# A four-layer trunk on one core: the delta-rule layer's matmuls put in one fixed order

## The chip, the core and the metric

The kernel runs on one core of a Trainium2 chip. The metric is the device time of one execution in microseconds (us), from launch to the last output. The profile is of one execution; its span runs from the first to the last instruction.

Engines: PE is TensorE (matmuls; PEld its weight loads), DVE is VectorE, ACT is ScalarE, POOL is GpSimd, SP is SyncE, which here only issues DMAs. Each engine takes its own instructions in order and waits on semaphores for what other engines make.

## The reference

Four residual layers on x (256 tokens by 1024, float32): pooling mixer, gated delta rule, latent attention, pooling mixer again; a final RMS norm. What matters here is layer 1, the delta-rule layer (8 heads, keys of 128, values of 256):

```
proj = h @ w_in                       # 1024 -> q 1024, k 1024, v 2048, gate 2048, b 8, a 8
qkv = silu(causal_depthwise_conv(qkv, conv_w))      # 4 taps
q, k = l2norm(q) * dk**-0.5, l2norm(k)
beta = sigmoid(b); g = cumsum(-exp(a_log) * softplus(a + dt_bias))   # within a chunk
L = strict_lower((k*beta) @ k.T * decay)
sol = triangular_solve(I + L, [v*beta, k*beta*exp(g)])
# per chunk, with a state per head:
v_new = u - w @ state
o = (q*exp(g)) @ state + (q @ k.T * decay) @ v_new
state = state * exp(g_last) + k_dec.T @ v_new
y = (rmsnorm(o, norm_g) * silu(gate)) @ w_out
```

The reference uses chunks of 64; the kernel uses two chunks of 128 tokens (t = 0 and 1) and so one state per head.

## The kernel before

**Strips.** A projection is done in strips of 512 output columns (`project`, L131). Weights come through SP in pieces of 512 KB (two 128-row slices of a strip, one "unit", so four units to a strip of w_in; three buffers `raw`). `weights` (L97) splits each slice into a rounded high part on ACT (`whi`, L117) and the rest on DVE or POOL (`wlo`, L119; the argument `pool` says which slices go to POOL); nine of each are kept. Each product is then three matmuls: high by high, high by low, low by high (`mm3`, L126 to L129, for strips whose output has channels on the partitions, 96 matmuls of 256 columns; L167 for strips with tokens on the partitions, 48 matmuls of 512 columns). I call the first kind C strips (q, k, v) and the second R strips (the gates).

**The delta-rule layer** (`gdn_layer`, L535). There are twelve strips: gates g0 to g3 (R), keys k0 and k1, queries q0 and q1, values v0 to v3 (C). A C strip's result lies in two PSUM banks. `conv` (L628) applies the taps: one scaled copy on ACT and three multiply-adds on DVE for each of four channel groups, then a SiLU on ACT. For keys and queries `channels` (L659) then transposes on PE (L675), squares on ACT (L678) and sums on DVE (L679, `ssq`); POOL makes the norms (`power`, L657). `against` (L683) multiplies keys by keys (to LT) or keys by queries (to attnT) for four heads and both chunks (16 matmul records, L688), and DVE scales them into SBUF (L692) by the decay DT, which DVE and ACT make (L618, L626) from a broadcast by DMA.

**The inverse.** `substitution` (L712) inverts the 32 by 32 diagonal blocks of all heads: eight DMAs gather them out of LT (`d_l`, L718), one brings them back with a block to a partition (`Lb`, L721), POOL does 31 steps of a product and a subtraction (L726, L730), one DMA writes the result (`d_t`, L732) and eight put it in T (L736). All these DMAs are on SP's queue, between the weights. `inverses` (L787) then joins the blocks: `pairs` (L806, L812) and `whole` (L820, L824, L830) for each chunk, PE and DVE in turns.

**The heads.** `news` (L839) makes the first chunk's values; then eight heads go through five stages (L870 to L926): `state`, `unseen`, `second`, `outputs`, `finished`. `outputs` is followed by a norm on ACT (L209) and POOL (L900 to L903) and a product with the gate on DVE (L906); `finished` transposes on PE (L915) for the output projection (`layer_out`, L348).

**The order.** The program text sets the order by the list

```
order = "g0 k0 d a0 g1 k1 a1 s q0 v0 i v1 v2 q1 g2 u0 v3 u1 g3".split()
```

(d the decays, a `lower`, s `substitution`, i `inverses`, u `news`), followed by the heads' steps and the output projection. But a planner that simulates the engines decides each engine's order: it may take any instruction whose inputs it believes to be ready, and so it mixes strips, inverses and heads. Where it believes a result to be earlier than the chip has it, the instruction that needs it stands at the head of its engine's queue and all behind it wait. `later` adds an order on one engine by hand. Buffer counts of most pools are also the planner's.

Of the kernel before, what the change touches and what calls it, by code (L numbers as in the profile page):

```python
# [42 lines left out]
def trunk(ctx: ExitStack, tc: tile.TileContext, x, positions, norm_g, pool_w_in, pool_w_grp,  # L43
# [48 lines left out]

    mark = {}
# [32 lines left out]
    def mm3(o, lhs, rhs, start, stop):  # L126
        nc.tensor.matmul(o, lhsT=lhs[0], rhs=rhs[0], start=start, stop=False)  # L127
        nc.tensor.matmul(o, lhsT=lhs[0], rhs=rhs[1], start=False, stop=False)  # L128
        nc.tensor.matmul(o, lhsT=lhs[1], rhs=rhs[0], start=False, stop=stop)  # L129

    def project(src, ks, act, cols=CW, chan=False, tail=0, done=None, cuts=1,  # L131
                where="acc", pool=()):
# [13 lines left out]
        if chan:  # L146
            banks = [bank(acc if where == "acc" else aux, where) for _ in range(2)]
            for k0, n in ks:
                parts = unit(k0, n)
                for j in range(n):  # L150
                    k = k0 + j
                    for c in range(cols // P):
# [3 lines left out]
                            k == last and c % 2 == 1)  # L156
            return banks
# [3 lines left out]
        def rows(t, c, k0, n, parts):  # L161
            o, sl = banks[t][c][:, :width], slice(c * width, (c + 1) * width)
            for x, y in ((0, 0), (0, 1), (1, 0)) if n == 1 else ((0, None), (1, 0)):
                for j in range(n):
                    k = k0 + j
                    for z in (0, 1) if y is None else (y,):
                        nc.tensor.matmul(o, lhsT=act(k, t * P, P)[x], rhs=parts[j][z][:, sl],  # L167
# [4 lines left out]
        for u, (k0, n) in enumerate(ks):  # L172
# [7 lines left out]
            for t in range(NT):  # L180
                for c in range(cuts):
                    for one in now:
                        rows(t, c, *one)
                    if done and u == len(ks) - 1:
                        done(t, c, banks[t][c][:, :width])
        return [b[0] for b in banks]
# [82 lines left out]
    for _ in range(WARM):  # L269
        nc.tensor.transpose(ps[:, :P], ident, ident)  # L270
# [41 lines left out]
    class LayerIn(Normed):  # L312
# [6 lines left out]
        def feed(self, t):  # L319
            for c, h in enumerate(self.rest(t)):  # L320
                ps = bank(tps, "tp")
                for b in range(4):
                    nc.tensor.transpose(ps[:, b * P:(b + 1) * P], h[:, b * P:(b + 1) * P], ident)
# [24 lines left out]
    def layer_out(w, yT, ks, i):  # L348
# [7 lines left out]
        project(cols_of(w, 0), ks, yT, done=lambda t, c, ps: done(t, 0, ps))  # L356
# [19 lines left out]
    def turn_params():  # L376
# [13 lines left out]
        nc.tensor.transpose(ps[:, :P], rows, ident)  # L390
# [20 lines left out]
    def pool_layer(i, j, hT):  # L411
# [37 lines left out]
        def mixed(g, pT, gs):  # L449
# [15 lines left out]
            for a in range(2):  # L465
                ps = bank(tps, "tp")
                for b in range(2):
                    for t in range(NT):
                        c = 2 * a + b
                        nc.tensor.transpose(ps[:, b * S + t * P:b * S + (t + 1) * P],  # L470
# [25 lines left out]
    def gdn_setup():  # L496
# [21 lines left out]
        nc.tensor.transpose(ps[:, :P], crow, ident)  # L518
# [16 lines left out]
    def gdn_layer(i, j, hT):  # L535
# [15 lines left out]
        def gate(vi):  # L551
            banks = project(cols_of(w_in, 2 * GDN_QK + GDN_V + vi * CW), units(KD), hT,
                            pool=((0, 4), (7,), (3, 7), (7,))[vi])
# [5 lines left out]
        order = "g0 k0 d a0 g1 k1 a1 s q0 v0 i v1 v2 q1 g2 u0 v3 u1 g3".split()  # L559
        while order[0][0] == "g":  # L560
            gate(int(order.pop(0)[1]))
# [3 lines left out]
        for k in range(KD):  # L565
            for x, part in enumerate(hT(k, 0, S)):
                nc.tensor.matmul(ps[:32, :S], lhsT=bws[:, k].rearrange("p a c -> p (a c)"),
# [4 lines left out]
        for t in range(NT):  # L572
            nc.tensor.transpose(ps[:, t * 32:(t + 1) * 32], ba[:, t * P:(t + 1) * P],
# [23 lines left out]
        nc.tensor.matmul(ps[:, :M], lhsT=utri, rhs=flat(lga), start=True, stop=True)  # L597
# [655 lines left out]
```

## Time and profile before

| what | before |
|---|---|
| median of 3 runs | 859.88 us (859.83 to 860.01) |
| the profiled execution's own time | 859.14 us |
| its span | 857.4 us |
| mean granted TensorE clock | 0.990 |

The delta-rule layer's matmuls lie from about 178 to 403 us of the span. In the lists of the profile a row is: line, engine, operation, output<-inputs, shape, count, then times. In timelines the first two numbers are start and length in us; of merged rows the length is the time covered. In brackets stands how long the engine had been idle and what released it. "PEclk" is the TensorE clock that was granted, 1.00 being full speed.

### The profile page before, as it was taken

Reading aid. Unit: us, or ns where it says so; the run is one execution under the profiler, and the core shown is the slowest. Engines: PE = TensorE matmul, PEld = TensorE weight load, DVE = VectorE, ACT = ScalarE, POOL = GpSimd, SP = SyncE. Lnnn points to the kernel's source line nnn. Section 1 sums busy time; section 2 is a strip of 40 time slices with the busy share of each in tenths; the row PEclk is TensorE's granted clock in tenths of the full one; section 3 lists DMA queues with packets and bytes.
Section 4 is the critical chain, followed back from the end, with each engine's and each line's share of the span. In section 5 each row is a group of like instructions: output and inputs, shape, how many; then the busy total and the mean of one; then the engine's idle time right before and its main releaser. Section 6 shows DMA issues by size and latency. Waiting matters only on the chain.

```text
span 857.4 us, 16137 instructions
## 1 busy us (share of the span) xinstructions
PE 835.0 (97%) x5967; PEld 778.7 (91%) x5967; DVE 591.2 (69%) x1138; ACT 488.2 (57%) x1007; POOL 155.7 (18%) x292
## 2 busy tenths in 40 slices
PE   7999999999999969999999999999999999999996
PEld 6999998988999959888979998999989989999986
DVE  4589776456989665656577659778767668866852
ACT  5565555467857435555565654566555476555542
POOL 4000000233248941022212002000000210000012
PEclk9999999999999989999999999999999999999999
DMA  6765556546555462222547676743652547565551
GB/s 199 249 188 188 178 189 213 180 148 206 188 160 176 134 168 102 75 74 99 173 147 215 201 165 172 196 132 95 171 167 79 173 149 218 175 192 183 187 200 50
DMA packets 111288, 140.43 MB, mean 164 GB/s; under 512 B 23340, under 2 KB 53224, under 8 KB 111208
## 3 DMA queue, kind: packets, MB, share of 16 engines
q1 hardware_dynamic: 109056, 138.17, 53.1%
q8 instruction: 47, 0.77, 0.4%
q0 software_dynamic: 320, 1.06, 0.3%
q10 hardware_dynamic: 1832, 0.16, 0.2%
q14 instruction: 33, 0.27, 0.1%
HBM read 137.79 MB, written 1.58 MB: 163 GB/s over the span
## 4 chain that ended last, share of the span: by engine, by line
PE 85%; POOL 7%; DVE 2%; DMA 2%; issue 2%; ACT 1%; SPq 1%; POOLq 0%; ACTq 0%; DVEq 0%
PE acc L167 34%; PE acc L127 12%; PE acc L128 12%; PE acc L129 12%; POOL Tb L730 2%; POOL pr L726 2%; PE aux L127 2%; PE aux L128 2%; PE aux L129 2%; DVE h L303 1%; DMA gain<-in_norm_g_dram 1%; PE aux L688 1%; ACT junk L209 1%; PE aux L806 1%; PE tp L1165 1%
## 5 line engine op out<-in xcount | busy, mean ns | idle before, releaser
L119 DVE TENSOR_TENSOR wlo<-raw,whi 128x512 fp32r<-128x512 f32 (+1 forms) x491 | 338.6, 712 | 163.2 <-ACT whi L117 160.9
L117 ACT CAST whi<-raw 128x512 fp32r<-128x512 f32 (+1 forms) x508 | 301.4, 617 | 261.8 <-PE acc L167 89.8
L127 PE MATMUL acc<-hTh,whi 128*128 128x256 f32 x832 | 235.3, 283 | 1.0 <-DVE cv L636 1.0
L128 PE MATMUL acc<-hTl,whi 128*128 128x256 f32 x832 | 235.8, 283 | 0.0
L129 PE MATMUL acc<-hTh,wlo 128*128 128x256 f32 x832 | 234.7, 282 | 0.0
L127 PEld LDWEIGHTS acc<-hTh,whi 128*128 128x128 f32 x832 | 157.7, 190 | 1.8 <-issue 1.4
L128 PEld LDWEIGHTS acc<-hTl,whi 128*128 128x128 f32 x832 | 157.6, 189 | 0.4
L129 PEld LDWEIGHTS acc<-hTh,wlo 128*128 128x128 f32 x832 | 157.5, 189 | 0.2
L167 PE MATMUL acc<-wlo,yTh 128*128 128x256 f32 (+1 forms) x384 | 116.2, 319 | 0.0
L167 PE MATMUL acc<-whi,yTh 128*128 128x256 f32 (+1 forms) x384 | 116.2, 323 | 0.0
L167 PE MATMUL acc<-whi,yTl 128*128 128x256 f32 (+1 forms) x384 | 92.4, 321 | 0.0
L167 PEld LDWEIGHTS acc<-wlo,yTh 128*128 128x128 f32 x384 | 72.0, 188 | 5.0
L167 PEld LDWEIGHTS acc<-whi,yTh 128*128 128x128 f32 x384 | 71.9, 188 | 5.2
L167 PEld LDWEIGHTS acc<-whi,yTl 128*128 128x128 f32 x384 | 63.1, 188 | 5.6
L291 POOL TENSOR_TENSOR hg<-x,gain 128x256 f32<-128x256 f32 x18 | 14.8, 832 | 259.1 <-DVE x L353 257.4
L167 PE MATMUL acc<-wlo,hTh 128*128 128x512 f32 (+1 forms) x144 | 55.9, 394 | 0.4 <-DVE wlo L119 0.2
L167 PE MATMUL acc<-whi,hTh 128*128 128x512 f32 (+1 forms) x144 | 55.5, 393 | 0.7 <-ACT hTh L195 0.7
L167 PE MATMUL acc<-whi,hTl 128*128 128x512 f32 (+1 forms) x144 | 45.4, 388 | 0.0
L119 POOL TENSOR_TENSOR wlo<-raw,whi 128x512 fp32r<-128x512 f32 x17 | 23.1, 1360 | 70.2 <-ACT whi L117 70.2
L434 POOL COPY win<-u 128x4 f32<-128x4 f32 x8 | 2.8, 354 | 177.0 <-ACT u L428 177.0
L167 PEld LDWEIGHTS acc<-wlo,hTh 128*128 128x128 f32 x144 | 27.3, 190 | 6.8 <-DVE wlo L119 1.7
L167 PEld LDWEIGHTS acc<-whi,hTh 128*128 128x128 f32 x144 | 27.3, 190 | 6.8 <-ACT hTh L195 1.7
(337 smaller groups left out, 1443.3 us busy)
## 6 DMA issues: line engine op xcount, KB each, us to landing
raw<-in_pool_w_in_dram SPq DMA_DIRECT2D x60, 512.0 KB, 4.4
raw<-in_gdn_w_in_dram SPq DMA_DIRECT2D x48, 512.0 KB, 3.9
raw<-in_pool_w_out_dram SPq DMA_DIRECT2D x32, 512.0 KB, 3.7
raw<-in_mla_w_in_dram SPq DMA_DIRECT2D x24, 512.0 KB, 4.4
raw<-in_mla_w_uq_dram SPq DMA_DIRECT2D x36, 256.0 KB, 3.8
raw<-in_pool_w_grp_dram SPq DMA_DIRECT2D x16, 512.0 KB, 4.2
raw<-in_gdn_w_out_dram SPq DMA_DIRECT2D x16, 512.0 KB, 3.5
raw<-in_mla_w_ukv_dram SPq DMA_DIRECT2D x32, 256.0 KB, 3.4
```

Of the source, the lines that this page charges most:

```text
L117: a = nc.scalar.copy(hi, v)
L119: b = e.tensor_tensor(out=lo, in0=v, in1=hi.bitcast(F32), op=ALU.subtract)
L127: nc.tensor.matmul(o, lhsT=lhs[0], rhs=rhs[0], start=start, stop=False)
L128: nc.tensor.matmul(o, lhsT=lhs[0], rhs=rhs[1], start=False, stop=False)
L129: nc.tensor.matmul(o, lhsT=lhs[1], rhs=rhs[0], start=False, stop=stop)
L167: nc.tensor.matmul(o, lhsT=act(k, t * P, P)[x], rhs=parts[j][z][:, sl], start=k == first and x == z == 0, stop=k == last and x == 1)
L209: nc.scalar.activation(junk[:, :n], src, AF.Square, scale=scale, accum_out=o)
L291: nc.gpsimd.tensor_tensor(out=self.early[t, a], in0=xs[t][:, sl], in1=self.g[:, sl], op=ALU.mult)
L303: nc.vector.scalar_tensor_tensor(out=h[:, cut:], in0=xs[t][:, sl], scalar=r[:, 0:1], in1=self.g[:, sl], op0=ALU.mult, op1=ALU.mult)
L688: nc.tensor.matmul(ps[:, b], lhsT=kT[hf][:, b, tt], rhs=rhs[hf][:, b, tt], start=True, stop=True)
L726: nc.gpsimd.tensor_tensor(out=pv, op=ALU.mult, in0=Lb[:, r, r + 1:, None].to_broadcast([M * Q, n, c]), in1=Tb[:, r:r + 1, :c].to_broadcast ...
L730: nc.gpsimd.tensor_tensor(out=tv, in0=tv, in1=pv, op=ALU.subtract)
```

## The change

From the second key strip on, every PE instruction of the layer, up to the first half of its output projection, is kept in the order of the program text (`pinned`, `keep_in_program_order`: each is placed behind the one traced before it on PE). The text's order is new and written out by unit: `project` is now a generator, and after each unit of a strip it runs the steps given for that place. The other engines' orders are still the planner's, and so is PE's outside the layer.

```diff
+    def matmul(*args, **opts):
+        ins = nc.tensor.matmul(*args, **opts)
+        return tc.keep_in_program_order(ins) if pinned["on"] else ins
...
+    def project(*args, between=(), **opts):
+
+        steps = strip(*args, **opts)
+        between = list(between)
+        while True:
+            try:
+                next(steps)
+            except StopIteration as end:
+                return end.value
+            side = between.pop(0) if between else None
+            for one in side or ():
+                one()
...
-        order = "g0 k0 d a0 g1 k1 a1 s q0 v0 i v1 v2 q1 g2 u0 v3 u1 g3".split()
...
+        keys(0)
+        decays()
+        pinned["on"] = True
+        keys(1, (), (), [do(key_norms, 0)])
+        queries(0, [do(lower, 0)], [do(key_norms, 1)], [do(lower, 1), substitution])
+        gate(1, (), [do(query_norms, 0)], [do(scored, 0)])
+        values(0)
+        queries(1, (), (), [do(values_turned, 0)])
+        gate(2, (), [do(query_norms, 1)], [do(scored, 1)])
+        values(1)
+        values(2, (), [do(values_turned, 1), inverses], [inv("pairs", 0)], [inv("pairs", 1)])
+        values(3, [inv("joined", 0)], [inv("joined", 1), inv("turned", 0)],
+               [do(values_turned, 2), inv("whole", 0), inv("turned", 1)],
+               [inv("last", 0), inv("whole", 1)])
+        gate(3, [inv("last", 1), do(news, 0)], [do(step, 0), do(values_turned, 3)],
+             [do(news, 1), do(step, 1)], [do(step, 2)])
+        for n in range(3, 6):
+            step(n)
+        return layer_out(gdn_w_out[j], yT, units(POOL_W // P), i,
+                         [[do(step, n)] for n in range(6, H + len(stages) - 1)])
```

`values(2, (), [x], [y], [z])` reads: strip v2, nothing after its first unit, x after the second, y after the third, z after the fourth. The old steps are cut into pieces that can be placed: `channels` into `channels` (strip, taps, SiLU) and `squares` (transposes, squares, sums; called by `key_norms` and `query_norms`, which also do POOL's norms); `queries` further into `scored` (the products with the keys); `values` into `values` and `values_turned`; `pairs` into `pairs` and `joined`; `whole` into `turned`, `whole`, `last`. `step(n)` does the five stages for heads n to n-4. `layer_out` puts steps 6 to 11 behind the first six units of its first half and then sets `pinned` off. `g0` and `k0` come before, in the planner's order.

The slices whose low part POOL makes also change:

```diff
-                            pool=((0, 4), (7,), (3, 7), (7,))[vi])
+                            pool=() if vi else (0, 4), between=between)
...
-                            pool=() if which else (0, 4))
+                            pool=() if which else (0, 2, 4, 6), between=between)
...
-                            pool=((1, 3, 5, 7), (3, 7), (), ())[vi])
+                            between=between)
```

The first is the gates, the second the keys (`which` is 0 for them), the third the values. Of the 96 slices of w_in POOL had sixteen and has ten; after k1 it has none. No arithmetic changes.

More of the change, by code (lines that the diff above doesn't have):

```diff
@@ L354, in done @@
             part_done(t, a, n)
-        project(cols_of(w, 0), ks, yT, done=lambda t, c, ps: done(t, 0, ps))
+        project(cols_of(w, 0), ks, yT, done=lambda t, c, ps: done(t, 0, ps), between=between)
+        pinned["on"] = False
         with later(mark["sp"]):
@@ L389, in turn_params @@
         ps = bank(tps, "tp")
-        nc.tensor.transpose(ps[:, :P], rows, ident)
+        transpose(ps[:, :P], rows, ident)
         nc.vector.tensor_copy(colsT, ps[:, :P])
@@ L853, in news @@
                                          scale=s1[:, 0, h:h + 1])
-        steps = {"g": gate, "k": keys, "a": lower, "q": queries, "v": values, "u": news}
-        once = {"s": substitution, "d": decays, "i": inverses}
-        for name in order:
-            if name in once:
-                once[name]()
-            else:
-                steps[name[0]](int(name[1]))
         yT = Split("yT", POOL_W // P)
```

160 lines of the change are left out of this document (90 added, 70 removed).

## The prediction

> **What bounds the kernel now.** I read the page first, then who waited for whom on PE inside the layer, then the windows around the longest wait, and last the timelines of PE, SP, POOL and DVE there.
>
> ```profile
> span 857.4 us, 16137 instructions
> PE 835.0 (97%) x5967; PEld 778.7 (91%) x5967; DVE 591.2 (69%) x1138; ACT 488.2 (57%) x1007; POOL 155.7 (18%) x292
> ```
>
> PE is busy for 97% of the span, so a new order can only win what PE loses by waiting or by a slower clock. In the layer's stretch, 180 to 403 us, the list of PE's waits has two rows:
>
> ```profile
> PE aux L806 <- DMA T<-d_t: 7.4, 1, 7.4
> PE acc L127 <- DVE cv L636: 1.0, 1, 1.0
> ```
>
> PE's timeline has both places, and the windows show the clock after the long one (their columns: PE, PEld, DVE, ACT, POOL, then PEclk):
>
> ```profile
> 303.87 0.36 PE L127 MATMUL acc<-hTh,whi 128*128 128x256 f32 x1 [0.97 <-DVE cv L636]
> 316.09 3.65 PE L806 MATMUL aux<-T,LT 128*128 128x64 f32 x16 [7.36 <-DMA T<-d_t]
> 326.57 1.89 PE L806 MATMUL aux<-T,LT 128*128 128x64 f32 x16
> ...
> 315.00:320.00 5.00, 3.91 (x18) 3.94 (x19) 3.38 (x4) 2.60 (x6) 0.00 (x0) 0.50 0.59 117
> 320.00:325.00 5.00, 5.00 (x29) 5.00 (x28) 1.50 (x3) 1.89 (x5) 0.00 (x0) 0.58 0.64 241
> 325.00:330.00 5.00, 5.00 (x50) 5.00 (x50) 2.67 (x5) 3.71 (x9) 0.00 (x0) 1.00 0.00 0
> ```
>
> `pairs` of the first chunk stood at the head of PE's queue for 7.36 us until T had landed. A good part of v3, the whole of g3 and the heads stood behind it, though they need no T or not yet. After the wait the clock was half: the sixteen matmuls of `pairs` took 3.65 us, and 1.89 us the second time. Half speed from 316.09 to 320 and a mean of 0.58 to 325 lose 0.5 x 3.91 + 0.42 x 5 = 4.05 us. So what can be won is 7.36 + 4.05 + 0.97 = 12.4 us. The profiled execution took 859.14 us, 1.74 more than its span and 0.74 (0.09%) less than the median, 859.88; I sum against 859.14. The floor is 859.1 - 12.4 = 846.7. About 0.2% (1.7 us) is what a measurement of this kernel can tell from no change.
>
> **The chain that T comes from,** on PE (its last product of keys by keys), SP and POOL:
>
> ```profile
> 238.10 0.61 PE L688 MATMUL aux<-kqT 128*128 128x128 f32 x4
> ...
> 256.10 0.53 SPq L721 DMA_DIRECT2D Lb<-d_l  x1
> 310.12 0.47 SPq L732 DMA_DIRECT2D d_t<-Tb  x1
> ...
> 259.78 0.23 POOL L726 TENSOR_TENSOR pr<-Lb,Tb 64x31 f32<-64x31 f32 x1 [1.25 <-DMA Lb<-d_l]
> 265.04 2.08 POOL L657 TENSOR_TENSOR rq<-rq,halves 128x8 f32<-128x8 f32 x1
> 293.13 1.28 POOL L119 TENSOR_TENSOR wlo<-raw,whi 128x512 fp32r<-128x512 f32 x1
> 298.81 1.29 POOL L119 TENSOR_TENSOR wlo<-raw,whi 128x512 fp32r<-128x512 f32 x1
> 309.85 0.24 POOL L730 TENSOR_TENSOR Tb<-Tb,pr 64x31 f32<-64x31 f32 x1
> 334.58 1.29 POOL L754 TENSOR_TENSOR Gb<-Gb,kqT 128x512 f32<-128x512 f32 x1 [1.02 <-ACT kqT L669]
> ```
>
> From the end of lower(1)'s matmuls (238.71) to T (316.09) are 77.4 us; 50.3 of them are POOL's (259.78 to 310.09), with foreign work between: one set of query norms (the `rq` row stands for it) and two weight slices. The change takes the slices out of the chain (-1.28 - 1.29). In the new order the second set of query norms falls into it in place of the first (no difference), with the 1.29 us product L754, which here came after. So the chain is 77.4 - 2.6 + 1.3 = 76.1 us.
>
> **What covers it after the change.** Rates of PE: a C strip, an R strip, sixteen matmuls of `against` (to the next row's start), eight transposes (the same):
>
> ```profile
> 270.00:280.00 10.00, 10.00 (x87) 10.00 (x86) 10.00 (x20) 6.39 (x13) 9.14 (x12) 1.00 0.61 179
> ...
> 204.60:213.00 8.40, 8.40 (x37) 6.75 (x36) 1.00 0.59 205
> ...
> 354.64 2.05 PE L688 MATMUL aux<-kqT 128*128 128x128 f32 x16
> 356.53 0.81 PE L847 MATMUL aux<-vR,U 128*128 128x256 f32 x3
> ...
> 352.55 1.09 PE L778 MATMUL tp<-ident,vc 128*128 128x128 f32 x8
> 353.57 0.62 PE L830 MATMUL aux<-U,X 64*64 64x64 f32 x7
> ```
>
> A C strip is 96 x 10/87 = 11.0 us, an R strip 48 x 8.4/37 = 10.9, `against` for four heads 1.89, eight transposes 1.02. Between lower(1) and pairs(0) the fixed order has: a quarter of q0, v0, q1, v1 and three quarters of v2, which is four C strips (44.0); g1 and g2 (21.8); `scored` twice (3.8); `query_norms` twice and `values_turned` twice (4.1). That is 73.7 us. T then comes 76.1 - 73.7 = 2.4 us late. PE waits 2.4 us there, with v2's last unit, v3 and the inverse queued behind. A gap of 0.97 us (above) left the clock at full rate, one of 7.36 did not; I take 2.4 with the short one and charge nothing for the clock.
>
> [...]
>
> Bounds of the wait: 0 (T early wins nothing, since PE is then busy), and about 7 where DVE scales LT later than now.
>
> **Keys back to back.** Both key strips and q0 now follow each other, with no R strip between, and PE must find each SiLU done at a fixed place. DVE's rows (twelve taps at the first row's rate, weight slices, half the decays, sum and copy for two heads, LT for four heads):
>
> ```profile
> 230.75 2.42 DVE L636 SCALAR_TENSOR_TENSOR cv<-acc,tap,cv 128x254 f32<-128x254 f32 x6
> 218.95 1.90 DVE L119 TENSOR_TENSOR wlo<-raw,whi 128x512 fp32r<-128x512 f32 x3
> 214.14 2.19 DVE L618 SCALAR_TENSOR_TENSOR DT<-Gb,G,maskT 128x128 f32<-128x128 f32 x8 [2.33 <-DMA Gb<-d_g]
> 220.75 0.68 DVE L679 TENSOR_REDUCE ssq<-sq 128x4 f32<-128x512 f32 x1
> 221.35 0.42 DVE L681 COPY ktok<-tp 128x256 f32<-128x256 f32 x1
> 225.88 2.16 DVE L692 SCALAR_TENSOR_TENSOR LT<-aux,s,DT 128x128 f32<-128x128 f32 x8
> ```
>
> A strip's taps are 4.8 us, a slice 0.63, the decays 4.4, a half's sums and copies 2.2, LT for four heads 2.2. While k1 runs (11.0 + 1.0 us) DVE has k0's taps, four slices of k1 and, early, four of q0: 4.8 + 8 x 0.63 = 9.8, which fits. After k1's end PE has two units and lower(0), 2 x 2.75 + 1.9 = 7.4 us, before it needs k1's SiLU for key_norms(1). If DVE takes k1's taps first, 4.8 fits; if the decays and the first sums go ahead, 4.4 + 2.2 + 4.8 = 11.4, and PE waits 4.0. I take 1.5, nearer to the first, since the decays can wait for LT. This wait delays chain and cover alike, so it adds. query_norms(0) comes two R units (5.4 us) after q0, with 4.8 of taps and up to 2.2 + 2.2 of sums and LT ahead of them on DVE: a wait of 0 to 4. It lies under the chain and comes off the 2.4 us at T; I add nothing.
>
> POOL now takes eight slices of the keys instead of four; the trace has one beside a slice of DVE:
>
> ```profile
> 242.31 1.30 POOL L119 TENSOR_TENSOR wlo<-raw,whi 128x512 fp32r<-128x512 f32 x1
> 242.39 1.76 DVE L119 TENSOR_TENSOR wlo<-raw,whi 128x512 fp32r<-128x512 f32 x1
> ```
>
> DVE's slice took 1.76 us instead of 0.63. For k1 that is at worst 4 x 1.1 = 4.5 us more on DVE, against 2 x 0.63 = 1.3 saved by the two more slices that POOL takes there; DVE's slack of 2.2 us and the early slices of q0 take most of it, so it stays within the 0 to 4 above.
>
> [...]
>
> **The heads.** Steps 3 to 5 have no unit between. `outputs` of a head must pass ACT, POOL and DVE before `finished`:
>
> ```profile
> 364.73 0.59 PE L895 MATMUL aux<-v,attnT 128*128 128x256 f32 x2
> 367.75 0.60 PE L869 MATMUL aux<-u,ktok 128*128 128x256 f32 x2
> ...
> 368.06 0.88 DVE L906 SCALAR_TENSOR_TENSOR yg<-aux,or,gsg 128x256 f32<-128x256 f32 x2 [1.35 <-POOL or L903]
> ```
>
> From 365.32 to 368.94 are 3.6 us. PE's work between, the next step's first four stages, is 2.6 (365.17 to 367.75 holds the same six products). One wait of 1.0 us in step 4; step 5 then has 0.4 more work between and that wait, and waits no more. The other steps have units of 2.75 us between. The inverse's pieces each have one or two units for their trip over DVE or ACT, so they add none. PE's instructions are the same in number, and the 0.97 us wait goes with the two POOL slices that held weights back.
>
> **Sum.** 859.1 - 12.4 + 1.5 (keys) + 2.4 (T) + 1.0 (heads) = 851.6 us.
>
> **The rivals.**
> - *The T wait stays.* The planner has no cause to hurry LT if it thinks POOL's chain shorter than it is, as it did before (it placed `pairs` 7.4 us early). If q0's taps (4.8 us) go ahead of LT(1), T is 2.4 + 4.8 = 7.2 us late and the clock's 4.05 is lost again: 851.6 + 4.8 + 4.05 = 860.4, no change. For it: two thirds of the chain is POOL's, and the planner took T for earlier than it was. Against: LT(1) needs only 2.2 us of DVE, and q0's taps become ready a unit (2.75 us) after lower(1). If half of that delay comes, 4.8 us late with half the clock's loss, it is 851.6 + 2.4 + 2.0 = 856.0.
> - *Slower: q0's taps as late as now.* Before, q0's taps and SiLU ran so:
>
> ```profile
> 241.88 0.48 DVE L636 SCALAR_TENSOR_TENSOR cv<-acc,tap,cv 128x255 f32<-128x255 f32 x1 [1.32 <-ACT cv L633]
> 254.85 0.47 DVE L636 SCALAR_TENSOR_TENSOR cv<-acc,tap,cv 128x253 f32<-128x253 f32 x1
> 255.86 1.33 ACT L669 ACTIVATE kqT<-cv 128x256 f32<-128x256 f32 x4
> ```
>
> From the first tap to the last SiLU are 15.3 us. Nothing waited then, as PE had other strips; in the fixed order query_norms(0) waits at 5.4 us, so 9.9 us with g1's second half behind it, and the clock halves (4.05). That hides the T wait: 859.1 - 12.4 + 1.5 + 9.9 + 4.05 + 1.0 = 863.2. It decides where the waits pass 12.4 us in all. Against it: those 15.3 us held twelve taps, LT and slices that nobody hurried; DVE's own sum is under 10.
> - *POOL's slices of the keys hold DVE up in full:* 3.2 us more at key_norms, 851.6 + 3.2 = 854.8. The pair of rows speaks for it, DVE's slack in k1 against; 0.12 of the forecast's 0.60, in whose own range it lies.
> - *The order binds nothing*, the planner having had nearly this one: 859. Unlikely, as the strips change places.
>
> **How the numbers follow.** The forecast has 0.60, with a range of its own from 847 to 855.5 (keys 0 to 4, T 0 to 3, heads 0 to 1.5). The T wait by half (856.0) 0.13; in full, with the order that binds nothing, 0.10, within 0.2%; slower 0.14; better than 847 0.03. Faster 0.76, same 0.10, slower 0.14. Left out above 860 are most of the slower cases and some of the full T wait; the range is 846.7 to 860.
>
> **What would show it.** [...] Wrong if a wait on kqT or on T is over 5 us and PEclk falls to 0.5 behind it. POOL's chain from the first `pr` to the last `Tb` should be about 49 us with no weight slice in it, and d_t should leave some 11 us sooner than now, since g1's strip (10.9 us) no longer lies ahead of lower(1).

## The result, and the profile after

| what | before | after |
|---|---|---|
| median | 859.86 us (859.09 to 860.01, 4 runs) | 885.7 us (884.45 to 886.94, 4 runs) |
| ratio to before, 95% interval | | 1.0308 (1.0293 to 1.0322) |
| span of the profiled execution | 857.4 us | 885.2 us |
| its mean granted TensorE clock | 0.990 | 0.975 |

The change makes the kernel 25.8 us slower. (One execution each of two kernels of the experiments, e6_late2 with 1656.44 us and e18_fit with 4475.5 us, stood far outside all others; the ratios leave it out, and the medians would move by under 0.2 us without it.) The page's head has nearly as many instructions as before, and PE busy for 9.9 us more (half clock counts as busy) in a span that is 27.8 us longer:

```profile
span 885.2 us, 16118 instructions
PE 844.9 (95%) x5967; PEld 784.7 (89%) x5967; DVE 594.7 (67%) x1144; ACT 494.6 (56%) x1009; POOL 144.1 (16%) x286
```

PE's waits between 180 and 410 us (total, times, longest):

```profile
PE tp L100 <- ACT kqT L694: 19.7, 9, 6.2
PE tp L100 <- ACT vc L810: 6.7, 3, 3.6
PE tp L100 <- DVE yg L948: 0.7, 1, 0.7
```

The row for T is gone, and so is the wait for a PSUM bank (`acc`). In their place 26.4 us stand at twelve transposes (L100 is the one line of all transposes now) that wait for a SiLU on ACT. PE's timeline gives the places:

```profile
213.05 1.30 PE L100 MATMUL tp<-ident,kqT 128*128 128x128 f32 x6 [2.96 <-ACT kqT L694]
218.68 0.69 PE L100 MATMUL tp<-ident,kqT 128*128 128x128 f32 x2 [4.33 <-ACT kqT L694]
...
233.81 0.82 PE L100 MATMUL tp<-ident,kqT 128*128 128x128 f32 x4 [1.83 <-ACT kqT L694]
...
252.66 0.66 PE L100 MATMUL tp<-ident,kqT 128*128 128x128 f32 x4 [1.09 <-ACT kqT L694]
...
285.98 0.66 PE L100 MATMUL tp<-ident,vc 128*128 128x128 f32 x4 [1.92 <-ACT vc L810]
...
301.29 0.69 PE L100 MATMUL tp<-ident,kqT 128*128 128x128 f32 x2 [6.21 <-ACT kqT L694]
...
332.83 0.66 PE L100 MATMUL tp<-ident,vc 128*128 128x128 f32 x4 [1.22 <-ACT vc L810]
337.07 1.12 PE L100 MATMUL tp<-ident,vc 128*128 128x128 f32 x4 [3.58 <-ACT vc L810]
```

In order they are `key_norms(0)` (two rows), `key_norms(1)`, `query_norms(0)`, `values_turned(0)`, `query_norms(1)` and `values_turned(1)` (two). No wait is over 6.21 us, yet the windows have the clock at half in several stretches (PE, PEld, DVE, ACT, POOL, PEclk, then the DMA share and GB/s):

```profile
215.00:220.00 5.00, 1.32 (x6) 1.33 (x7) 5.00 (x16) 4.08 (x5) 0.00 (x0) 0.50 0.42 130
235.00:240.00 5.00, 4.68 (x22) 4.68 (x23) 2.97 (x9) 1.48 (x3) 1.93 (x2) 0.50 0.21 79
300.00:305.00 5.00, 2.12 (x8) 1.32 (x9) 2.33 (x4) 2.97 (x7) 1.17 (x5) 0.50 0.50 133
```

In the first PE worked 1.32 us of 5; in the second it worked 4.68 us at half clock behind a wait that was over. Half clock while PE stands is not counted as a loss here. Counted in windows of 1 us, and only for the time that PE works, half clock costs 4.0 us before and 12.3 us after. With the waits (8.4 and 27.1 us, all rows between 180 and 410 us) that is 27.0 of the 27.8 us.

Why was a SiLU late? At `key_norms(0)` DVE shows it:

```profile
213.61 2.19 DVE L643 SCALAR_TENSOR_TENSOR DT<-Gb,G,maskT 128x128 f32<-128x128 f32 x8 [1.90 <-DMA Gb<-d_g]
215.72 0.68 DVE L130 TENSOR_TENSOR wlo<-raw,whi 128x512 fp32r<-128x512 f32 x1
216.32 0.47 DVE L661 SCALAR_TENSOR_TENSOR cv<-acc,tap,cv 128x253 f32<-128x253 f32 x1
```

The last tap of k0 (216.32) stood behind half the decays, which themselves waited 1.90 us for the broadcast Gb. The SiLU then ran at 218.21, behind ACT's Exp (1.06 us) and two table loads (1.28 us each). At `values_turned(0)` nothing is wrong but the place: the taps need 4.8 us, and DVE made six weight slices for PE among the twelve of them, so that they took from 275.3 to 285.2. At `values_turned(1)` it was so too, and the last tap of v1 stood behind the first step of the inverse as well, which the text sets right behind this place:

```profile
333.56 2.36 DVE L841 STREAM_TRANSPOSE U<-T 128x1024 f32<-128x1024 f32 x2
335.85 0.44 DVE L661 SCALAR_TENSOR_TENSOR vc<-acc,tap,vc 128x253 f32<-128x253 f32 x1
```

At `query_norms(1)` ACT's row is:

```profile
300.82 0.72 ACT L694 ACTIVATE kqT<-cv 128x256 f32<-128x256 f32 x2 [7.60 <-POOL pr L756]
```

The SiLU's input had long been there. POOL's last `pr`, the last reader of Lb, ends at 300.79, and in the compiled program q1's kqT lies on the bytes of Lb (106688 to 110784). So it looks like a wait for memory, which e9_lbown tries below.

### The profile page after: what moved, and what is told of

It is laid out like the page before. It is cut to its first block, busy times and chain, and to the rows that moved or that the text cites. A ratio compares the mean times of both kernels' runs of the same rounds, so it can differ in the third digit from the quotient of the medians.

```text
span 885.2 us, 16118 instructions
## 1 busy us (share of the span) xinstructions
PE 844.9 (95%) x5967; PEld 784.7 (89%) x5967; DVE 594.7 (67%) x1144; ACT 494.6 (56%) x1009; POOL 144.1 (16%) x286
## 3 DMA queue, kind: packets, MB, share of 16 engines
q0 software_dynamic: 320, 1.06, 0.4%
## 4 chain that ended last, share of the span: by engine, by line
PE 83%; POOL 6%; DVE 4%; DMA 2%; ACT 2%; issue 2%; SPq 0%; POOLq 0%; ACTq 0%; DVEq 0%
PE acc L96 68%; PE aux L96 12%; PE tp L100 3%; POOL Tb L760 2%; POOL pr L756 2%; DVE wlo L130 1%; DVE h L329 1%; DMA raw<-in_gdn_w_in_dram 1%; DMA gain<-in_norm_g_dram 1%; DMA Lb<-d_l 1%; DVE cv L661 1%; ACT junk L235 0%; ACT whi L128 0%; POOL xr L322 0%; DVE x L379 0%
## 5 line engine op out<-in xcount | busy, mean ns | idle before, releaser
L130 DVE TENSOR_TENSOR wlo<-raw,whi 128x512 fp32r<-128x512 f32 (+1 forms) x497 | 342.3, 710 | 190.2 <-ACT whi L128 181.7
L96 PEld LDWEIGHTS acc<-hTh,whi 128*128 128x128 f32 x832 | 159.5, 192 | 0.8
L96 PEld LDWEIGHTS acc<-hTl,whi 128*128 128x128 f32 x832 | 159.5, 192 | 0.4
L96 PEld LDWEIGHTS acc<-hTh,wlo 128*128 128x128 f32 x832 | 159.4, 192 | 0.1
L96 PE MATMUL acc<-whi,hTh 128*128 128x512 f32 (+1 forms) x144 | 58.6, 413 | 0.7 <-ACT hTh L221 0.7
L96 PE MATMUL acc<-wlo,hTh 128*128 128x512 f32 (+1 forms) x144 | 58.1, 407 | 0.5 <-DVE wlo L130 0.2
L96 PEld LDWEIGHTS acc<-whi,hTl 128*128 128x128 f32 x144 | 27.6, 195 | 5.9 <-DVE hTl L226 0.2
```

What stands on the lines that cost most here:

```text
L96: ins = nc.tensor.matmul(*args, **opts)
L130: b = e.tensor_tensor(out=lo, in0=v, in1=hi.bitcast(F32), op=ALU.subtract)
```

## The experiments

Each was timed beside the kernel before on its own chip. "Waits" are the rows of PE's list between 180 and 410 us added up; "clock" is 5 us x (1 - PEclk) over that stretch's 46 windows of 5 us, so it counts half clock under a wait too. Both are from the profiled execution, whose time can lie off the median: by 3.9 us in e1_free, 3.6 in e6_late2, 2.9 in e12_keyslate.

| kernel | median us | ratio, 95% interval | span | waits | clock |
|---|---|---|---|---|---|
| before | 859.86 | | 857.4 | 8.4 | 5.2 |
| after | 885.7 | 1.0308 (1.0293 to 1.0322) | 885.2 | 27.1 | 17.1 |
| e1_free | 863.8 | 1.005 (1.0029 to 1.0072) | 866.0 | 13.8 | 11.9 |
| e2_lb | 886.16 | 1.0309 (1.0288 to 1.0331) | 883.6 | 28.1 | 15.3 |
| e3_late | 860.33 | 1.0012 (0.9995 to 1.0028) | 857.1 | 8.5 | 3.4 |
| e4_pool | 881.84 | 1.0261 (1.0241 to 1.028) | 879.8 | 23.9 | 11.9 |
| e5_lbkept | 889.13 | 1.0345 (1.0331 to 1.0359) | 887.4 | 29.6 | 15.4 |
| e6_late2 | 869.63 | 1.011 (1.0094 to 1.0125) | 871.4 | 13.6 | 8.6 |
| e7_hold | 863.94 | 1.0053 (1.0041 to 1.0066) | 862.2 | 8.6 | 10.3 |
| e8_late2free | 865.12 | 1.0064 (1.005 to 1.0077) | 863.5 | 14.4 | 10.3 |
| e9_lbown | 882.89 | 1.0265 (1.025 to 1.0279) | 881.2 | 24.4 | 15.4 |
| e10_lower | 864.41 | 1.0048 (1.0035 to 1.0061) | 863.1 | 14.7 | 5.2 |
| e11_pairs | 869.15 | 1.0104 (1.0085 to 1.0123) | 865.7 | 12.0 | 10.3 |
| e12_keyslate | 880.51 | 1.0245 (1.0227 to 1.0262) | 881.7 | 25.2 | 13.6 |
| e15_qafter | 884.78 | 1.0293 (1.0279 to 1.0306) | 883.0 | 29.8 | 13.6 |
| e16_qbefore | 862.74 | 1.0043 (1.0028 to 1.0059) | 860.5 | 9.1 | 8.6 |
| e17_q11 | 864.11 | 1.0048 (1.0034 to 1.0062) | 862.0 | 8.8 | 8.6 |
| e18_fit | 860.64 | 1.0018 (1.0005 to 1.0032) | 860.9 | 6.1 | 10.3 |
| e19_lateq | 864.98 | 1.0058 (1.0046 to 1.007) | 863.2 | 13.9 | 6.8 |
| e20_beforeq | 859.99 | 1.0000 (0.9991 to 1.0009) | 858.4 | 8.8 | 5.1 |

In all twenty kernels the span less waits and clock is 838.9 to 849.2 us. With half clock counted only while PE works, as above, it is 842.8 to 850.2, and 843.7 to 846.6 in seventeen of them: PE's waits and its clock in this layer account for the differences to within 3 us there. The other three are e8_late2free (842.8), e12_keyslate (847.6) and e6_late2 (850.2).

### Is it the pin or the places?

**e1_free** leaves PE to the planner, in the new text order:

```diff
-        pinned["on"] = True
```

> The changed kernel with PE's order left to the planner (nothing pinned); text order, cut steps and POOL's slices stay as changed. If the 27 us of waits at the transposes and the half clock behind them come from the fixed places, they go: 846 to 862 us, with at most 3 us of waits on kqT and vc together, perhaps again a wait on T. If the new text order (keys and q0 back to back) or the other share of POOL is to blame, it stays over 870.

Measured 863.8, between the two ranges. PE's list:

```profile
PE aux L96 <- DMA T<-d_t: 11.2, 1, 11.2
PE tp L100 <- ACT kqT L694: 2.2, 1, 2.2
PE aux L96 <- ACT sq L705: 0.4, 1, 0.4
```

The waits on SiLUs fall from 26.4 to 2.2 us, but T is late again, by 11.2. The text, the pieces and POOL's slices are those of the kernel after; only the pin is gone, and with it 21.9 us. Unpinned, PE can fill a late SiLU with other work.

**e3_late** keeps the pin and moves the places later (key and query norms 14 to 19 us behind their strips, the inverse by a strip):

```diff
-        keys(1, (), (), [do(key_norms, 0)])
-        queries(0, [do(lower, 0)], [do(key_norms, 1)], [do(lower, 1), substitution])
-        gate(1, (), [do(query_norms, 0)], [do(scored, 0)])
...
+        keys(1)
+        queries(0, (), [do(key_norms, 0)], (), [do(lower, 0)])
+        gate(1, (), [do(key_norms, 1)], (), [do(lower, 1), substitution])
+        values(0, (), [do(query_norms, 0)], [do(scored, 0)])
+        queries(1)
+        gate(2, [do(values_turned, 0)])
+        values(1, (), (), [do(query_norms, 1)], [do(scored, 1)])
+        values(2)
+        values(3, [do(values_turned, 1)], [inverses, inv("pairs", 0)], [inv("pairs", 1)],
+               [inv("joined", 0)])
...
```

> Still pinned, Lb in memory of its own, and every step that transposes a strip set about a strip later (14 to 19 us after its strip's end instead of 5 to 9); the inverse one strip later too. If only the places were too early, the waits at the transposes go and PEclk stays at 1: 848 to 856, with up to 4 us of waits at T or between the last heads' steps. If a fixed order costs in itself (other engines planned badly around it), it stays over 862.

Measured 860.33, 25 us under the kernel after, and 4 us above the range. PE's list:

```profile
PE aux L96 <- DMA T<-d_t: 5.0, 1, 5.0
PE acc L96 <- DVE ktok L708: 2.8, 1, 2.8
PE tp L100 <- DVE yg L948: 0.7, 1, 0.7
```

With the same instructions pinned, not one transpose waits for a SiLU. So neither the pin nor the text cost the 25 us by itself: the text unpinned costs 4 us (e1_free), the pin with later places 0.5 us, which is within the noise, and early places under the pin 25.8. (Lb is in the pool `const` here, as in e2_lb, and in the kernels made from this one.) No SiLU waits for POOL here, so the wait for memory is gone as well. What this text does not do is beat the kernel before: T is 5.0 us late again.

**e12_keyslate** moves only the places of the keys and of q0 in the kernel after:

```diff
-        keys(1, (), (), [do(key_norms, 0)])
-        queries(0, [do(lower, 0)], [do(key_norms, 1)], [do(lower, 1), substitution])
-        gate(1, (), [do(query_norms, 0)], [do(scored, 0)])
+        keys(1)
+        queries(0, (), [do(key_norms, 0)], (), [do(lower, 0)])
+        gate(1, (), [do(key_norms, 1)], [do(lower, 1), substitution, do(query_norms, 0)],
+             [do(scored, 0)])
```

> The kernel after; only the places of the keys and of the first query half are later (key_norms(0), lower(0), key_norms(1), lower(1), query_norms(0), as many as 14 us behind their strips); those of the values, of the second query half and of the inverse stay. Theory (each place too near its strip costs its own wait, and its own spell of half clock): the six waits at key_norms and query_norms(0), 13.9 us together, go, and the three spells of half clock between 213 and 258 us; left are values_turned(0) 2.2, query_norms(1) 4 to 9, values_turned(1) 5.3 and the heads 1.0, with 4 to 8 us of clock: 864 to 872 us. Rival (the fixed order itself costs, wherever the places are, since nothing can fill a wait): the waits move to other places, 878 to 886.

Measured 880.51: the theory missed by 8.5 us or more, and the rival's number was right. At the moved places 1.2 us are left, but PE waits 5.1 us for a bank whose taps DVE hasn't done, and the values' transposes wait 14.7 us instead of 6.7, 7.92 of it at one place. There ACT stood 4.84 and 4.46 us for weights, with the SiLU behind it. The waits of one place are not its own: repair one, and PE comes sooner to the next.

### Which other causes?

**e4_pool** gives POOL the weight slices that it has in the kernel before:

```diff
-                            pool=() if vi else (0, 4), between=between)
+                            pool=((0, 4), (7,), (3, 7), (7,))[vi], between=between)
...
-                            pool=() if which else (0, 2, 4, 6), between=between)
+                            pool=() if which else (0, 4), between=between)
...
-                            between=between)
+                            pool=((1, 3, 5, 7), (3, 7), (), ())[vi], between=between)
```

> The changed kernel with POOL's slices as before (sixteen, six of them in the values). If moving slices from POOL to DVE made the taps late, the waits at values_turned and query_norms shrink and it is faster by over 5 us: 875 to 880. If not, 882 to 895: slices in the middle of POOL's chain make Lb and T later.

Measured 881.84, about 4 us better than the kernel after, and between the two ranges. No SiLU of q1 waits for POOL's `pr` here, so the lost wait for memory is in those 4 us as well; the two were not separated.

**e2_lb** and **e5_lbkept** were to take Lb off the bytes of q1's kqT, by another pool (`const`) and by a late read of one element of it:

> The changed kernel with Lb (the gathered blocks that POOL reads) in memory of its own. In the changed kernel the SiLU of q1's first channels started right after POOL's last read of Lb (300.8 after 300.8), 7.6 us after ACT stood idle. If kqT of q1 lay in Lb's memory, PE's wait at query_norms(1) falls from 8 us to 0 to 2, its half clock goes, and the time is 873 to 879. If the SiLU was late through DVE's taps alone, nothing changes: 884 to 887.

> The changed kernel with Lb read once more (one element to a partition, DVE) where the inverses begin, after q1's SiLU, so that no other tile can be laid into its memory; in the run with Lb in another pool the SiLU of q1 still started right after POOL's last read of Lb (298.45 after 298.42), so the memory may have been shared there too. If shared memory held that SiLU back, the 8 us wait at query_norms(1) shrinks to the 1 to 3 us that the taps alone cost, and the time is 873 to 880. If not, 883 to 887.

Measured 886.16 and 889.13. Neither was a test: in both, ACT's row for q1's first SiLU still waits for POOL's last `pr` (9.06 and 5.79 us), so the planner goes on laying kqT where Lb was. Nothing made the read of e5_lbkept late; why it is 3.4 us slower than the kernel after was not looked for. **e9_lbown** adds that element to U, which needs T:

```diff
...
+            nc.vector.tensor_tensor(out=seen, in0=held["Lb"][:, 0, :1], op=ALU.add,
+                                    in1=U[1][:M * Q, 0, :1])
```

> The kernel after; Lb now stays alive until the inverses (one element of it is added to U there), so that in the compiled program the second query half's kqT no longer lies on Lb's bytes (addresses 106688 to 110784 before, 127168 now). Theory (q1's SiLU waits until POOL's last step has read Lb, since it writes onto Lb): the row of kqT released by POOL's pr (7.6 us of idle ACT) goes, the wait of 6.6 us at query_norms(1) falls to the 3.4 us that it had with the other slices on POOL, some of the half clock behind it (299 to 309 us) goes, 878 to 882 us in all. Rival (the second query half's taps on DVE are what is late, and POOL's pr only happens to end then): the wait stays at 6 to 7 us, 884 to 888.

Measured 882.89, 2.8 us better, and 0.9 above the range of the theory. kqT is now at 127168, and ACT's rows for the same SiLUs no longer name POOL:

```profile
292.39 0.41 ACT L694 ACTIVATE kqT<-cv 128x256 f32<-128x256 f32 x1
293.91 0.42 ACT L694 ACTIVATE kqT<-cv 128x256 f32<-128x256 f32 x1 [1.11 <-DVE cv L661]
```

PE's waits at `query_norms(1)` fall from 7.8 us (6.21 + 0.96 + 0.62) to 2.8 (1.17 + 1.67). That the wait was for memory is shown; it was worth 5.0 us there, of which `values_turned(1)` took 2.8 back.

### Why do later places not win the 12 us?

**e6_late2** (pinned; g1 between k1 and q0, `pairs` a unit later than e3_late) and **e8_late2free** (the same, not pinned) tried another late order; **e7_hold** takes the kernel before, unpinned, and holds the inverse on PE behind v3:

```diff
-        order = "g0 k0 d a0 g1 k1 a1 s q0 v0 i v1 v2 q1 g2 u0 v3 u1 g3".split()
+        order = "g0 k0 d a0 g1 k1 a1 s q0 v0 v1 v2 q1 g2 v3 i u0 u1 g3".split()
...
+                with later(strip["last"]):
+                    inverses()
```

> Pinned, the turned steps 14 to 19 us behind their strips as in the first late version, but g1 between k1 and q0 (so that LT of the second half stands beside no taps on DVE), Lb kept, and pairs one unit later. If waits at too early places are all that a fixed order costs, what is left is a wait at T of 0 to 3 us and about 1 us between the heads: 847 to 852 us, faster than both kernels. If a fixed order has a cost of its own, 857 or more.

> The text of the second late version with nothing pinned. If pinning is what keeps pairs behind the strips, the planner pulls pairs forward again, and a wait on T of 5 to 12 us with half clock behind it is back: 855 to 866. If the text order alone does it, within 2 us of the pinned one.

> The kernel before with one change: the inverses are traced behind v3 and held on PE behind v3's last matmul; nothing pinned. If the kernel before lost its time only because the planner put pairs ahead of work that was ready, the wait at T falls from 7.4 to 0 to 2 us and the half clock goes: 847 to 852 us. If the planner finds another early place to wait, 856 or more.

Measured 869.63, 865.12 and 863.94. The hoped-for times of e6_late2 and e7_hold missed, and the ranges of their rivals hold; e8_late2free lies in its first range, but without the wait for T that was to give it. None of the three waits for T. With this text the pin itself costs 4.5 us (e6_late2 against e8_late2free). e6_late2 waits 1.3 to 2.5 us at seven places, e8_late2free 9.5 us at `values_turned(1)`. In e7_hold the pieces of the inverse lie bare behind v3, with waits of 0.7 to 0.9 us, and the clock is half from 349 to 362 us; two more waits, of 2.9 and 1.9 us, stand at q1's SiLU and at a gate.

Then **e10_lower** sets lower(1) two units sooner than e3_late, **e11_pairs** the inverse two units later:

```diff
-        gate(1, (), [do(key_norms, 1)], (), [do(lower, 1), substitution])
+        gate(1, (), [do(key_norms, 1), do(lower, 1), substitution])
```

```diff
-        values(3, [do(values_turned, 1)], [inverses, inv("pairs", 0)], [inv("pairs", 1)],
-               [inv("joined", 0)])
+        values(3, [do(values_turned, 1)], (), (), [inverses, inv("pairs", 0)])
...
```

> The kernel of e3_late; lower(1) and the substitution stand right behind key_norms(1), two units of g1 (5.5 us) sooner. Theory (what was left of e3_late's time is the 5.0 us wait for T and the 3.4 us that half clock costs behind it): d_t leaves about 5 us sooner, the wait on T falls under 1 us, the half clock at 318 to 325 goes, 852 to 854 us, faster than before. Rival (DVE sends LT(1) no sooner, as it still has q0's taps and the weight slices, or POOL's chain gets slower): T lands less than 2 us sooner, 858 to 861.

> The kernel of e3_late; all pieces of the inverse two units (5.5 us) later, so that last and news are laid bare behind g3. Theory: the 5.0 us wait for T goes, with the 3.4 us of clock; the pieces that now follow each other behind g3 (whole, last, news, with trips over DVE and ACT of 0.7 to 1.2 us between them) add 2 to 3 us; 854 to 856 us. Rival (the trips behind g3 cost as much as the wait, and let the clock fall there): 859 to 863.

Measured 864.41 and 869.15, above all ranges. The wait for T goes in both, and one of 9.9 us (for v1's SiLU) and of 7.1 us (for a bank) stands in its place. In e10_lower d_t left no sooner (315.44 instead of 313.25), as the rival had it; but the lost time came from elsewhere. ACT's timeline of e10_lower:

```profile
305.39 0.63 ACT L810 ACTIVATE vc<-vc 128x512 f32<-128x512 f32 x1
320.69 1.14 ACT L128 CAST whi<-raw 128x512 fp32r<-128x512 f32 x2 [14.67 <-DMA raw<-in_gdn_w_in_dram]
321.73 0.63 ACT L810 ACTIVATE vc<-vc 128x512 f32<-128x512 f32 x1
```

The SiLU that PE wanted stood on ACT behind the rounding of a weight slice that had not come. It had not come because SP, which loads the weights, stood at d_t for the end of POOL's chain. SP's list of waits in e10_lower, then in e11_pairs (X is cleared on POOL right behind the chain's last step):

```profile
SPq L762 <- POOL X L840: 18.6, 1, 18.6
```

```profile
SPq L762 <- POOL X L840: 12.7, 1, 12.7
```

**e17_q11** is e11_pairs with d_t and the loads of T on POOL's own DMA queue; **e15_qafter** and **e16_qbefore** do that to the kernels after and before:

```diff
-            nc.sync.dma_start(out=d_t.rearrange("m (r c) -> m r c", r=B), in_=Tb)
+            nc.gpsimd.dma_start(out=d_t.rearrange("m (r c) -> m r c", r=B), in_=Tb)
...
-                    nc.sync.dma_start(out=T[t][d * B:(d + 1) * B, :, d * B:(d + 1) * B],
+                    nc.gpsimd.dma_start(out=T[t][d * B:(d + 1) * B, :, d * B:(d + 1) * B],
```

> The kernel of e11_pairs; d_t and the loads of T on POOL's DMA queue. In e11_pairs SP stood 12.7 us at d_t, ACT then 11.3 us for a weight slice, and PE 7.1 us for a bank whose taps came late. Theory (d_t on SP holds back the weights, and PE waits for those): SP's row for Tb and the 7.1 us go, with the half clock at 325 to 335 that costs 3.4; 857 to 860 us. Rival (DVE or the banks are what is late at 324 us, whatever the weights do): the wait stays over 4 us, 864 to 870.

Measured 864.11, 5.0 us under e11_pairs and at the lower end of the rival's range. ACT's waits for weights of w_in fall from 17.2 us (longest 11.3) to 4.0 (1.5), and the 7.1 us for a bank to 2.1:

```profile
PE acc L96 <- DVE ktok L708: 2.8, 1, 2.8
PE aux L96 <- DMA T<-d_t: 2.4, 1, 2.4
PE acc L96 <- DVE vc L661: 2.1, 1, 2.1
```

So d_t on SP did hold back the weights. But half of the expected gain is missing: T is again what PE waits for. POOL took 0.584 us to issue a load of T where SP took 0.446 (e3_late; both are medians of eight). The move to POOL's queue saved PE a 7.1 us wait in part (2.1 us are left), because the issue that waited, 12.7 us on SP, held the weight loads behind it.

> The kernel after; d_t and the eight loads of T are issued on POOL's DMA queue instead of SP's, where d_t stood for 11.0 us at the head until POOL's chain had ended, with the next weight slices behind it. Theory (in the kernel after it is the places of the transposes that cost; the held-up weights lie under those waits): the waits on kqT and vc stay, 883 to 887 us. Rival (the weights behind d_t on SP are what makes the values' SiLU late): the waits at values_turned(1) (1.2 and 3.6 us) go with their half clock, 876 to 880.

> The kernel before; d_t and the loads of T on POOL's DMA queue. Theory: T is late there because POOL's chain ends late, not because of the queue, so the wait on T stays at 6 to 9 us and the time within 0.3% of before, 857.5 to 862. Rival (the 4.8 us that SP stood at d_t held back weights that PE then had to wait for): the time falls by 2 us or more, under 857.5.

Measured 884.78 and 862.74. In the kernel after the queue is not the cause: the waits at `values_turned(1)` stay at 1.21 and 3.58 us. In the kernel before it makes 0.43% more, 0.7 us above the theory's range. SP had stood there for only 4.8 us, and POOL issued the loads of T from 315.7 us on, SP from 313.1; but PE's wait for T is 6.4 us, not longer than before, and what the rest comes from was not tried.

**e18_fit** sets the inverse of e17_q11 for both chunks together, one piece behind v3 and behind each unit of g3:

```diff
...
+        values(3, [do(values_turned, 1)], (), (), [inverses, inv("pairs", 0), inv("pairs", 1)])
+        gate(3, [inv("joined", 0), inv("joined", 1)],
+             [do(values_turned, 2), inv("turned", 0), inv("turned", 1)],
+             [inv("whole", 0), inv("whole", 1)], [inv("last", 0), inv("last", 1)])
...
```

> As e17_q11, with the five pieces of the inverse set for both chunks together, behind v3's last unit and each of g3's four units, so that none is laid bare behind g3. Theory: T is there (landed about 320 us, pairs at about 320), no wait over 1 us but the one at 231 us (2.8, with 1.7 of clock) and yg (0.7), no half clock at 355 to 366 us; 851 to 855 us, faster than before. Rival (T lands over 3 us behind v3's end, since POOL issues the eight loads more slowly than SP did): a wait on T of 3 to 5 us and half clock behind it, 857 to 861.

Measured 860.64, in the rival's range: the fewest waits of all (6.1 us), but 10.3 us of clock. Behind the 2.35 us for T the clock was half from 325 to 335 us. It fell behind the wait of 2.8 us at 231 us too, though not behind the same wait in e3_late (the first fence is e3_late, the second e18_fit; in the windows PEclk stands third from the end):

```profile
230.58 0.47 PE L96 MATMUL acc<-whi,hTh 128*128 128x512 f32 x1 [2.81 <-DVE ktok L708]
...
230.00:235.00 5.00, 4.42 (x19) 3.62 (x20) 5.00 (x12) 3.84 (x10) 2.29 (x2) 1.00 0.66 205
```

```profile
231.10 0.47 PE L96 MATMUL acc<-whi,hTh 128*128 128x512 f32 x1 [2.82 <-DVE ktok L708]
...
230.00:235.00 5.00, 3.90 (x12) 3.17 (x13) 4.64 (x11) 2.87 (x8) 1.88 (x2) 0.76 0.75 210
```

So behind a wait of this length the clock was 1.00 in one run and 0.76 in the other over the same 5 us; no run shows what decides. And in e18_fit the clock fell once more with no wait ahead:

```profile
345.92 4.64 PE L96 MATMUL aux<-T,LT 64*128 64x64 f32 x32
```

```profile
345.00:350.00 5.00, 5.00 (x36) 0.86 0.33 113
350.00:355.00 5.00, 5.00 (x14) 0.50 0.01 5
```

(The second fence has PE alone, then PEclk, the DMA share and GB/s.) Thirty-two small matmuls in a row (64 rows, 64 columns each) ran there, with PE "busy" throughout. PEclk was 1.00 over 345 to 348 us and 0.60 over 348 to 351, so the clock went from full to half at about 348.6 us, among them. In e11_pairs and e7_hold the clock was half over the same pieces of the inverse (0.50 over 355 to 365 and over 350 to 360 us), with no wait over 0.9 us. In e3_late the same matmuls went sixteen at a time with strips between (2.00 us each time), and the clock stayed full (1.00 over 342 to 357 us). That the small matmuls are the cause was not tried by itself.

**e19_lateq** and **e20_beforeq** shorten POOL's chain itself, in e3_late and in the kernel before: POOL's part of the query norms waits for the chain's end.

```diff
+            with later(mark["chain"]):
+                nc.gpsimd.tensor_tensor(out=ev, in0=ev, in1=qT[hf][:, :, P:], op=ALU.mult)
...
-                            pool=((1, 3, 5, 7), (3, 7), (), ())[vi])
+                            pool=((1, 3, 5, 7), (), (), ())[vi])
```

(The last two lines are of e20_beforeq alone.)

> The kernel of e3_late; POOL's part of both query norms (the product onto Gb and the scales rq) may start only behind the last step of the substitution. In e3_late 3.9 us of it lay inside POOL's chain. Theory (in the late order POOL's chain is what is left: PE waits 5.0 us for T, and half clock costs 3.4 behind it): d_t leaves about 4 us sooner, the wait for T is 0 to 1.5 us, the half clock at 318 to 325 goes; 851 to 854 us, faster than before. Rival (something else is as late as T at 314 to 319 us, the weights that stand behind d_t on SP above all, so another wait takes its place): 857 to 861.

> The kernel before; the same edit of the query norms, and the two weight slices of v1 that POOL split (1.28 and 1.29 us, inside its chain) go to DVE: 5 to 6 us of foreign work out of the chain. Theory (the chain's length sets the 7.4 us wait for T, and the order needs no pin): d_t leaves 5 to 6 us sooner, the wait for T falls to 1 to 3 us with less half clock behind it; 850 to 855 us. Rival (with nothing pinned the planner moves pairs forward by what it takes the chain to be shorter, or puts other work late): the wait on T stays over 4 us or another takes its place, 857 to 861.

Measured 864.98, above both ranges, and 859.99, in the rival's. In e19_lateq d_t left at 312.85, 0.4 us sooner instead of 4, since the chain had begun later (Lb was issued at 260.49, not 257.68); SP stood 16.0 us, ACT 14.3 for a weight, and PE 9.5 for v1's SiLU, so the rival's mechanism was right. In e20_beforeq the slices that I took off POOL were not the two inside the chain, which are still there at 294.03 and 301.53; d_t left 1.2 us sooner, and T's wait fell from 7.4 to 6.5. No version here beats the kernel before.

## Why the prediction was wrong

**The failed step is "Keys back to back", with all that it left out.** It asked at two places whether PE finds its SiLU done: `key_norms(1)`, for 1.5 us (0 to 4), and `query_norms(0)`. The waits at the first are 2.5 (1.83 + 0.68), inside that range. But the change pins eight such places on PE, of which six waited, and `key_norms(0)` (7.3), `values_turned(0)` (1.9), `query_norms(1)` (7.8) and `values_turned(1)` (4.8) were put at nothing: 21.8 of the 26.4 us. The row of the decays, with 2.33 us of waiting for Gb, was quoted; I put it into DVE's sum for k1 and not ahead of k0's last tap. I also summed DVE's work as if it ran in one piece, while DVE interleaves taps with slices that PE needs at once: 4.8 us of taps took 9.9 at v0 and 10.2 at k1 (224.65 to 234.82).

**query_norms(0)** (0 to 4) waited 2.1, as bounded. But it was to come off the wait at T, and there was none: the 2.1 us added in full.

**"I charge nothing for the clock"** failed with it. I judged each wait alone, 0.97 us free and 7.36 not, and put 2.4 with the free one: an estimate from these two waits alone. In e18_fit a wait of 2.35 us was followed by half clock for 10 us. In the kernel after the clock fell behind one wait of 2.96 us (at 213.7 us), behind one of 1.83 (at 234.2), and behind two of 1.09 and 1.04 with four transposes between (at 254.6). The loss while PE works went from 4.0 to 12.3 us. The length of a single wait does not sort these cases: one of 2.81 us left the clock full in e3_late, and in e18_fit the clock was 0.50 over 350 to 355 us, where PE did not stand.

**The T wait** was forecast at 2.4 us and was 0: the waits ahead of it held PE back until `pairs` came at 341.7, some 31 us behind T's landing. POOL's chain had no slice in it and took 47.2 us (forecast about 49); d_t left at 301.14, 9.0 us sooner than before (forecast some 11). That part of the mechanism was right, and it bought nothing. The whole chain, from the end of lower(1)'s matmuls to T, was forecast at 76.1 us and took 67.8 (242.91 to about 310.7), as POOL's part began 11.0 us behind lower(1) instead of 21.1: it was shorter than the 73.7 us of cover, so by these numbers the 2.4 us would have been 0 without the other waits too. Where the SiLU waits are gone (e3_late), T is late by 5.0 us.

**The heads** cost 0.7 (forecast 1.0). Put into the sum, SiLU waits of 26.4 instead of 1.5, clock of 12.3 instead of 0, T at 0 instead of 2.4 and this 0.7 make 34.5 of the 35.3 us between 851.6 and the profiled execution's 886.94.

**POOL's key slices** as a rival (3.2 us): e4_pool puts all of POOL's slices back at once, the keys' included, and gains about 4 us, the wait for memory in it; what the keys' slices alone cost DVE stays open.

**The slower rival had the mechanism but one place only:** "q0's taps as late as now" for 9.9 us and 4.05 of clock. At q0 it was 2.1; over six places it was 26.4, with more clock, so 885.7 instead of 863.2. That this rival pointed the right way was in part luck: its one place was not where the time went. What the text named as proof against it came true at q1: a wait on kqT over 5 us with PEclk at 0.5 behind it.

**The 12.4 us that could be won** did not come in any version. Each order that frees PE of one wait brings it sooner to the next thing that is late: SiLUs, then T, then the weights behind d_t on SP, or the clock over the inverse's small matmuls. That d_t holds the weights is shown (e17_q11); why the chain starts later in each late order was read from SP's rows and not tested.

## What to carry to other kernels

Before an engine's order is fixed, list every instruction in it that waits for another engine, and for each compare the slot with how long that result took in the trace of before, start to end, interleaved work included; there is no filler any more, so the shortfalls come as waits (26.4 us at twelve transposes here), with half clock on top (12.3 us instead of 4.0). A place that has slack in engine time can still be late by memory reuse (5.0 us at `query_norms(1)`, e9_lbown) or by a queue that also issues other DMAs (SP stood 12.7 us at d_t with weights behind it, e11_pairs): look for who last read the bytes it writes, and for what stands ahead of its loads. When a repaired wait returns as another one elsewhere, add up waits and clock over the whole stage, not over the place.

## What the runs showed of the hardware that was not expected

- Half clock without a wait: among thirty-two small matmuls (e18_fit) PEclk fell from 1.00 (345 to 348 us) to 0.50 (350 to 355 us), with PE busy for 5.00 of 5 us.
- The same wait of 2.8 to 2.9 us on PE left the clock full in e3_late (PEclk 1.00 over 230 to 235 us) and was followed by half clock in e11_pairs, e17_q11, e18_fit and e19_lateq (0.72, 0.66, 0.76 and 0.66 over the same 5 us).
- ACT loaded a function table four times between 211 and 221.4 us of the kernel after, 1.28 us each, as SiLU and Exp took turns; two of them lay between k0's third SiLU and its last.
- The same DMA took 0.584 us to issue on POOL and about 0.446 on SP (loads of T, e17_q11 and e3_late).
